# Three transformer blocks with a mixture of experts: two more pieces of expert weights on chip, a top-64 on 32 partitions, wider modulation sums and a final norm by 128 tokens

## The chip, the cores and the metric

The kernel runs on one core of one Trainium2 chip. The metric is device time in microseconds, median of three runs. Engines: PE (matmuls), DVE (vector), ACT (activations, and one queue of DMA issues), POOL (a few vector operations and the indirect gathers), SP (the other queue of DMA issues). A traced execution gives the rows below; its times count from the start of its span.

## The reference, cut to what matters

Two transformer blocks in a row on 512 tokens of width 1024 (mLSTM and MLP, then short convolution and MLP), and then a third with modulation, attention and a mixture of 16 experts. The parts that the diff touches belong to the third:

```
mod = silu(c) @ w_mod + b_mod            # 1024 -> 6144; the same with c_ctx for the context (only 2048 columns are used)
...
x = x + g_a * mix                        # mix = attention output projection
h2 = rmsnorm(x, norm_ffn) * (1 + sc_f) + sh_f
aff = softmax(h2 @ w_router)             # 512 tokens x 16 experts
vals, idx = top_k(aff.T, 64)             # every expert takes its 64 best tokens
xs = h2[idx]                             # 16 x 64 x 1024
y = (silu(xs @ w_gate) * (xs @ w_up)) @ w_down * vals     # per expert: 1024 -> 512 -> 1024
x = x + g_f * scatter_add(y, idx)
return rmsnorm(x, norm_final)
```

All data are float32.

## The kernel before

The program is traced as ordinary loops; a framework then places the instructions on each engine. It takes the instruction that stands first in the program among those that it expects to be ready by its own estimates of durations, so the order on an engine can differ from the program's, and buffers are taken and freed by tag. `keep_in_program_order` pins an instruction.

*Dense stages.* Activations lie with the channels on 128 partitions and 512 tokens on columns. Every weight piece is loaded by SP into `raw`, and split by ACT (L85) and DVE (L86) into a high and a low part `wh`, `wl`; three matmuls (L92 to L94) make one product.

*Modulation (`mods`, L829).* The vector product is not made on PE. For each j of 24 blocks of 256 columns, DVE accumulates 8 slices of `w_mod` times a column of silu(c) into `u` (L877 and L881; twice for the first 8 blocks, since the context needs them too). Loads go in pieces of four slices into tag `b4`. Every four sums, PE adds over partitions with a column block of ones (`rows`), and the sums are turned into columns. The generator's steps are taken between the MLP's blocks, so all this lies beside the matmuls of the first two blocks.

*Attention's output (`attention_out`, L1382).* For each of the 8 channel blocks k: a product, the residual on DVE (L1427), the router's partial sums `stats` on PE (L1402), and the square of x on ACT, added to `acc` by POOL or, for the last two, by DVE (L194, L196). Then `colsum` (L207) makes four columns of sums of squares on PE, `rstd_cols` the reciprocal roots, and L1433 the logits `lg`, with tokens on partitions (4 blocks of 128 tokens, 16 experts each).

*Routing (`route`, L1437).* Softmax; four transposes (L1452) to experts on 16 partitions and 512 tokens on columns, copied into `aT`; eight rounds of the 8 largest values and their replacement by -1 (L1478, L1480); four transposes back (L1485); `sel` marks what was replaced (L1487); triangular and full matmuls (L1489, L1491) count the rank of each token chosen; `rank` (L1494). `onehots` (L1507) compares ranks with 0 to 63, `slots` (L1517) makes each slot's token number, weight and address by matmul, `fetch` (L1529) gathers the 128 token rows of a pair of experts from `h2d` in HBM. Beside this, PE transposes the normalized tokens back to rows (L1472), ACT scales them (L1473) into one tile of tag `ha` and three of tag `wh`, and ACT's queue writes them to `h2d` (L1474).

*Experts (`moe`, L1562).* 8 pairs of experts. Per pair: `feed` transposes the gathered rows (L1573) and modulates them into `xs`; `half` (L1626) makes the gate and up products in halves of four slices, two experts in the two 64-column halves of PE; `inner` (L1632) transposes the activations; `down` (L1605) makes the output of the pair before; `weigh` (L1612, L1613) scales and splits it; `scatter` (L1587, L1588) multiplies with a one-hot and adds into x. The program asks for a pair's second `half` after the scatter of the pair before.

*Expert weights (`moe_loads`, L1532).* 96 pieces of 1 MB (four slices of 512 columns), in the order of use, issued by SP, one buffer each. `mwtags` lists the tags: 10 `mw`, 1 `mx` (that is given back after the routing), 2 `raw`, 2 `mz`. Fifteen pieces are asked for before `route`; the sixteenth takes the first buffer that PE has read, and after `mx` has gone the ring has 14 buffers. The final norm's weights `nf` and a tile `gf` have tag `wh`; `nf` is loaded by ACT's queue (L1675).

*End.* The last pair's output is made in four blocks j of 256 columns with the tokens on partitions (L1595), added to x by two matmuls per 128 tokens, with the high and the low part in turn (L1718, L1719); ACT squares and sums (L1721). Behind the last block: one sum over all four token blocks (L1726), one root (L1727), one reciprocal (L1728), then for each 128 tokens half a row scaled on ACT (L1731), half on DVE (L1732), and a store by SP or ACT's queue (L1733).

Of the kernel before, what the change touches and what calls it, by code (L numbers as in the profile page):

```python
# [18 lines left out]
S = 512  # L19
D = 1024  # L20
# [7 lines left out]
class Net:  # L28
# [800 lines left out]
    def mods(self):  # L829
# [5 lines left out]
        ones = self.c([128, 32], name="ones32")  # L835
        nc.gpsimd.memset(ones, 1.0)
# [24 lines left out]
        for j in range(24):  # L861
            nv = 2 if j < 8 else 1
            if len(sums) % 2 == 0:
                pair = self.t([128, 2, 256], tag="u")
            if nv == 2:
                acc = [pair[:, 0], pair[:, 1]]
            else:
                acc = [pair[:, len(sums) % 2]]
            sums += acc
            for hf in range(2):  # L870
                raw = self.t([128, 4, 256], tag="b4")
                nc.sync.dma_start(raw, a["w_mod_2"][0][hf * 512:(hf + 1) * 512, j * 256:(j + 1) * 256].rearrange("(k p) n -> p k n", p=128))
                for v in range(nv):
                    for k in range(4):
                        c = cs[:, v, hf * 4 + k:hf * 4 + k + 1]
                        if hf + k == 0:
                            o = nc.vector.tensor_scalar(acc[v], raw[:, k], c, None, op0=OP.mult)  # L877
                            if v == 0 and j % 2 == 0:
                                self.tc.keep_in_program_order(o)
                        else:  # L880
                            nc.vector.scalar_tensor_tensor(acc[v], raw[:, k], c, acc[v], op0=OP.mult, op1=OP.add)  # L881
            if j % 2:
                yield
                if len(sums) == 4:
                    t = rows(sums)
                    sums = []
                yield
                if t is not None:
                    columns(t, j, nv)
                    t = None  # L890
# [491 lines left out]
    def attention_out(self, oops):  # L1382
# [22 lines left out]
        for k in range(KD):  # L1405
# [22 lines left out]
            ss.add(self.x[:, k])  # L1428
        stats(KD - 1)
        cols, _ = self.colsum(ss.acc)  # L1430
# [6 lines left out]
    def route(self, cols, lg):  # L1437
# [49 lines left out]
        nc.vector.tensor_scalar(sel, pT[:, 0:64].rearrange("p (c e) -> p c e", c=4), 0.0, None, op0=OP.is_lt)  # L1487
        pp = self.p()[:, 0:64].rearrange("p (c e) -> p c e", c=4)
        nc.tensor.matmul(pp, tri[:, 0], sel, start=True, stop=False, skip_group_check=True)  # L1489
        for c in range(3):  # L1490
            nc.tensor.matmul(pp[:, c + 1:], tri[:, 1], sel[:, c:c + 1].to_broadcast([128, 3 - c, 16]), start=False, stop=c == 2,  # L1491
                             skip_group_check=True)
        rank = self.t([128, 4, 16], tag="rank")
# [5 lines left out]
        for pr in range(2):  # L1499
            self.slots(pr)  # L1500
            self.fetch(pr)
# [326 lines left out]
```

## Time and profile before

| | |
|---|---|
| median of 3 runs | 1812.56 us (1810.69 to 1812.74) |
| profiled execution, own time | 1812.28 us |
| its span | 1810.4 us, 24232 instructions |
| PE busy | 1747.0 us, 96% |
| DVE, ACT, POOL busy | 1009.1 (56%), 680.7 (38%), 80.5 us (4%) |
| chain that ended last | PE 90%, DVE 5%, ACT 3%, DMA 1% |
| moved by DMA | 254.47 MB, mean 141 GB/s |
| mean granted TensorE clock | 0.984 of full speed |

A busy share is a mean over the whole span. In the 40 slices of the page the DMA engines move 48 to 163 GB/s from slice 2 to the attention, 9 to 25 GB/s in most of the attention, and 417 to 420 in four slices of the experts' stage.

### The profile page before, as it was taken

The numbers are of one execution on the slowest core, as the hardware profiler recorded it, in microseconds if no ns is written. First come the engines' busy times: TensorE is split into PE (matmuls) and PEld (weight loads), VectorE is DVE, ScalarE is ACT, GpSimd is POOL, SyncE is SP. The second block draws the span as 40 slices with busy tenths as digits, with TensorE's granted clock in tenths as the row PEclk, the third lists the DMA queues.
The fourth block names the chain that finished last, engine by engine and source line by source line (L and its number), as shares of the span: only waits on it lengthen the run. The fifth ranks groups of instructions, "written<-read, shape, count | busy, mean of one in ns | idle before, by whom it ended". The sixth has DMA issues, their size and how long they took to land.

```text
span 1810.4 us, 24232 instructions
## 1 busy us (share of the span) xinstructions
PE 1747.0 (96%) x9763; PEld 1375.6 (76%) x9763; DVE 1009.1 (56%) x1930; ACT 680.7 (38%) x1228; POOL 80.5 (4%) x100
## 2 busy tenths in 40 slices
PE   7999999999999999999999999989899999799997
PEld 5798898777787888898787878888788887334444
DVE  4554575366756774536455554678776743433332
ACT  4344345333322442244323333344666642111112
POOL 1000000000000000000000001013000001000000
PEclk9899999999999999999999999989999999899999
DMA  6221432244544222322444333220100047799993
GB/s 196 71 70 48 147 110 93 94 140 140 163 140 140 94 93 94 116 93 94 139 140 139 120 105 105 70 75 12 25 13 9 20 142 302 272 419 420 420 417 123
DMA packets 157447, 254.47 MB, mean 141 GB/s; under 512 B 20223, under 2 KB 124056, under 8 KB 145432
## 3 DMA queue, kind: packets, MB, share of 16 engines
q1 hardware_dynamic: 152304, 244.70, 38.7%
q10 hardware_dynamic: 3528, 3.98, 0.7%
q0 software_dynamic: 1504, 4.26, 0.6%
q8 instruction: 76, 1.25, 0.3%
q14 instruction: 35, 0.29, 0.0%
HBM read 248.72 MB, written 4.20 MB: 140 GB/s over the span
## 4 chain that ended last, share of the span: by engine, by line
PE 90%; DVE 5%; ACT 3%; issue 1%; DMA 1%; SPq 0%; DVEq 0%; POOL 0%; ACTq 0%
PE ps L92 22%; PE ps L94 22%; PE ps L93 22%; PE ps L1626 7%; PE ps L1605 3%; PE ps L1185 2%; PE ps L1170 2%; PE pw L1323 1%; PE ps L1588 1%; PE pw L1322 1%; PE ps L1587 1%; ACT wh L85 1%; PE ps L1573 1%; DVE th L301 1%; PE ps L1595 0%
## 5 line engine op out<-in xcount | busy, mean ns | idle before, releaser
L92 PE MATMUL ps<-op,wh 128*128 128x512 f32 (+1 forms) x1808 | 653.3, 367 | 7.0 <-ACT wh L85 2.2
L94 PE MATMUL ps<-op,wl 128*128 128x512 f32 (+1 forms) x1808 | 657.9, 366 | 2.2 <-DVE wl L86 2.2
L93 PE MATMUL ps<-op,wh 128*128 128x512 f32 (+1 forms) x1808 | 658.0, 366 | 0.9 <-DVE op L105 0.7
L86 DVE TENSOR_TENSOR wl<-raw,wh 128x1024 fp32r<-128x1024 f32 x210 | 258.1, 1233 | 256.1 <-ACT wh L85 255.5
L92 PEld LDWEIGHTS ps<-op,wh 128*128 128x128 f32 x1808 | 338.1, 189 | 70.5 <-issue 3.3
L93 PEld LDWEIGHTS ps<-op,wh 128*128 128x128 f32 x1808 | 341.8, 189 | 61.3 <-DVE op L105 1.3
L94 PEld LDWEIGHTS ps<-op,wl 128*128 128x128 f32 x1808 | 341.7, 189 | 60.5 <-DVE wl L86 2.9
L85 ACT CAST wh<-raw 128x1024 fp32r<-128x1024 f32 x210 | 219.9, 1052 | 385.6 <-PE ps L93 350.1
L688 DVE TENSOR_TENSOR t<-t,ps 128x512 f32<-128x512 f32 x96 | 65.8, 686 | 112.0 <-PE ps L94 111.8
L1626 PE MATMUL ps<-mw,xs 128*64 128x512 f32 x400 | 115.3, 600 | 0.0
L881 DVE SCALAR_TENSOR_TENSOR u<-b,csilu,u 128x256 f32<-128x256 f32 x224 | 103.9, 492 | 7.7 <-DMA b<-in_w_mod_dram 3.9
L637 ACT ACTIVATE t<-ps 128x512 f32<-128x512 f32 x64 | 38.0, 594 | 109.0 <-PE ps L94 108.9
L92 PE MATMUL ps<-wh,op 128*128 128x256 f32 x256 | 75.3, 295 | 0.1
L1626 PEld LDWEIGHTS ps<-mw,xs 128*64 128x64 f32 x400 | 33.4, 138 | 52.9 <-issue 50.5
L93 PE MATMUL ps<-wl,op 128*128 128x256 f32 x256 | 72.4, 284 | 0.0
L94 PE MATMUL ps<-wh,op 128*128 128x256 f32 x256 | 71.7, 285 | 0.0
L1140 DVE TENSOR_REDUCE sm<-pw 128x1 f32<-128x768 f32 (+2 forms) x64 | 54.1, 854 | 27.4 <-PE pw L1323 14.2
L196 POOL TENSOR_TENSOR acc<-acc,t 128x512 f32<-128x512 f32 x21 | 28.1, 1337 | 605.4 <-ACT t L194 604.8
L92 PEld LDWEIGHTS ps<-wh,op 128*128 128x128 f32 x256 | 49.1, 192 | 4.2 <-ACT og L532 2.3
L93 PEld LDWEIGHTS ps<-wl,op 128*128 128x128 f32 x256 | 49.0, 192 | 0.2
L1580 DVE TENSOR_SCALAR xs<-ps,Ap 128x128 f32<-128x128 f32 x32 | 13.0, 408 | 64.5 <-PE ps L1573 57.3
L94 PEld LDWEIGHTS ps<-wh,op 128*128 128x128 f32 x256 | 48.3, 191 | 0.1
(467 smaller groups left out, 2158.7 us busy)
## 6 DMA issues: line engine op xcount, KB each, us to landing
raw<-in_w_mlp_up_dram SPq DMA_DIRECT2D x32, 1024.0 KB, 5.5
raw<-in_w_mlp_down_dram SPq DMA_DIRECT2D x32, 1024.0 KB, 5.0
mw<-in_w_gate_dram SPq DMA_DIRECT2D x26, 1024.0 KB, 16.6
b<-in_w_mod_dram SPq DMA_DIRECT2D x48, 512.0 KB, 4.7
mw<-in_w_up_dram SPq DMA_DIRECT2D x24, 1024.0 KB, 18.0
mw<-in_w_down_dram SPq DMA_DIRECT2D x19, 1024.0 KB, 19.9
raw<-in_w_in_conv_dram SPq DMA_DIRECT2D x12, 1024.0 KB, 5.1
raw<-in_w_in_mlstm_dram SPq DMA_DIRECT2D x11, 1024.0 KB, 5.4
```

The lines of the kernel that those rows point to most:

```text
L85: nc.scalar.copy(h, raw[:, k0:k0 + kk])
L86: (eng or nc.vector).tensor_sub(lo, raw[:, k0:k0 + kk], h.bitcast(F32))
L92: mm(out, st[0], mv[0], start=first, stop=False)
L93: mm(out, st[0], mv[1], start=False, stop=False)
L94: mm(out, st[1], mv[0], start=False, stop=last)
L637: nc.scalar.activation(t, src, AF.Relu)
L688: nc.vector.tensor_add(y[i], y[i], p)
L881: nc.vector.scalar_tensor_tensor(acc[v], raw[:, k], c, acc[v], op0=OP.mult, op1=OP.add)
L1140: nc.vector.reduce_max(nm[e], p[e][:, 256:256 + n], axis=AX.X, negate=self.sink is None)
L1170: nc.tensor.transpose(pt[:, x * 128:(x + 1) * 128], self.P[e][:, m * 128:(m + 1) * 128], net.ident)
L1605: nc.tensor.matmul(py[dh][e * 64:e * 64 + 64], aT[:, fh * 2 + f, e * 64:e * 64 + 64], r[e][:, f, dh * 512:dh * 512 + 512], start=fh + f == ...
L1626: nc.tensor.matmul(p[e * 64:e * 64 + 64], xs[:, k, e * 64:e * 64 + 64], r[e][:, k % 4], start=k == 0, stop=k == 7, tile_position=(0, e * 64))
```

## The change

- `mods`: blocks of 512 columns instead of 256 (12 blocks), loads of two slices of 512 columns instead of four of 256, one accumulating instruction over 512 columns. The tile of ones becomes a broadcast of one column.
- `attention_out`: the last block's square is no longer added to `acc`; PE sums the columns of `acc` and of the square into the same four columns.
- `route`: two transposes of 32 columns give 32 partitions (two blocks of 128 tokens, 16 experts each) with 256 columns. Eight maxima and seven replacements give each partition its 64 largest, in falling order. A matmul brings partitions 16 to 31 down to 0 to 15; the maximum of one list with the other reversed holds the 64 largest of both, and its minimum is the expert's threshold. It is spread by a transpose, and `lg` is compared with it: greater, and equal. Ranks are counted for both, those that are equal behind all that are greater.
- `onehots` can be made for two of four experts at a time, so the first pair's slots and gather stand ahead of the second pair's one-hots. `oh` has 4 buffers instead of 8.
- `moe_loads`: two more places in the ring, each of two half pieces: `ha` with `la`, and two of `wh`. They are free when the normalized tokens have been written out. They are used three times (the second place), four times (the first).
- The end: in each block the four matmuls of the high part stand before the four of the low part; sum, root, reciprocal and scaling are made for each 128 tokens.

The diff, cut where only shapes follow from what is shown:

```diff
-        for j in range(24):
+        for j in range(1, 24, 2):
             nv = 2 if j < 8 else 1
...
-            for hf in range(2):
-                raw = self.t([128, 4, 256], tag="b4")
-                nc.sync.dma_start(raw, a["w_mod_2"][0][hf * 512:(hf + 1) * 512, j * 256:(j + 1) * 256].rearrange("(k p) n -> p k n", p=128))
+            for k2 in range(KD // 2):
+                raw = self.t([128, 2, 512], tag="b4")
+                nc.sync.dma_start(raw, a["w_mod_2"][0][k2 * 256:(k2 + 1) * 256, (j - 1) * 256:(j + 1) * 256].rearrange("(k p) n -> p k n", p=128))
...
-                            nc.vector.scalar_tensor_tensor(acc[v], raw[:, k], c, acc[v], op0=OP.mult, op1=OP.add)
+                            nc.vector.scalar_tensor_tensor(o, raw[:, k], c, o, op0=OP.mult, op1=OP.add)
...
-            ss.add(self.x[:, k])
+            if k < KD - 1:
+                ss.add(self.x[:, k])
+        sq = self.t([128, S])
+        nc.scalar.activation(sq, self.x[:, KD - 1], AF.Square)
         stats(KD - 1)
-        cols, _ = self.colsum(ss.acc)
+        pc = self.p()
+        for n, src in enumerate((ss.acc, sq)):
+            for c in range(4):
+                nc.tensor.matmul(pc[:, c:c + 1], src[:, c * 128:(c + 1) * 128], self.ones, start=n + c == 0, stop=n == 1,
+                                 skip_group_check=True)
+        cols = self.rstd_cols(pc[:, 0:4], 4, 1.0 / D)
...
-        for c in range(4):
-            nc.tensor.transpose(pT[0:16, c * 128:(c + 1) * 128], lg[:, c], self.ident)
-        aT = self.t([16, S], tag="aT")
-        nc.vector.tensor_copy(aT, pT[0:16])
+        for i in range(2):
+            nc.tensor.transpose(pT[0:32, i * 128:(i + 1) * 128], lg[:, 2 * i:2 * i + 2].rearrange("p c e -> p (c e)"), self.ident)
+        aT = self.t([32, 256], tag="aT")
+        nc.vector.tensor_copy(aT, pT[0:32, 0:256])
...
-        wk = aT
+        wk, top = aT, self.sm([32, 64])
         for r in range(8):
-            v = self.sm([16, 8])
+            v = top[:, 8 * r:8 * r + 8]
             nc.vector.max(v, wk)
-            nw = self.t([16, S], tag="aT")
-            nc.vector.match_replace(out=nw, in_to_replace=v, in_values=wk, imm_value=-1.0)
-            wk = nw
+            if r < 7:
+                nw = self.t([32, 256], tag="aT")
+                nc.vector.match_replace(out=nw, in_to_replace=v, in_values=wk, imm_value=-1.0)
+                wk = nw
...
-        for c in range(4):
-            nc.tensor.transpose(pT[:, c * 16:c * 16 + 16], wk[:, c * 128:(c + 1) * 128], self.ident[0:16, 0:16])
-        sel = self.t([128, 4, 16], BF, tag="sel")
-        nc.vector.tensor_scalar(sel, pT[:, 0:64].rearrange("p (c e) -> p c e", c=4), 0.0, None, op0=OP.is_lt)
+        nc.tensor.matmul(pT[0:16, 0:64], self.ident[0:32, 16:32], top, start=True, stop=True)
+        m, th = top[0:16], self.sm([16, 1])
+        nc.vector.tensor_tensor(m, m, pT[0:16, 0:64][:, ::-1], op=OP.max)
+        nc.vector.tensor_reduce(th, m, axis=AX.X, op=OP.min)
+        pT = self.p()
+        nc.tensor.transpose(pT[:, 0:16], th.to_broadcast([16, 128]), self.ident[0:16, 0:16])
+
+        sel = self.t([128, 4, 2, 16], BF, tag="sel")
+        T = pT[:, 0:16][:, None, :].to_broadcast([128, 4, 16])
+        nc.vector.tensor_tensor(sel[:, :, 0], lg, T, op=OP.is_gt)
+        nc.vector.tensor_tensor(sel[:, :, 1], lg, T, op=OP.is_equal)
...
+        for c in range(4):
+            nc.tensor.matmul(pp[:, :, 1], tri[:, 1], sel[:, c:c + 1, 0].to_broadcast([128, 4, 16]), start=False, stop=c == 3,
+                             skip_group_check=True)
+        both = self.t([128, 4, 2, 16])
+        nc.vector.tensor_mul(both, pp, sel)
         rank = self.t([128, 4, 16], tag="rank")
-        nc.vector.tensor_mul(rank, pp, sel)
+        nc.vector.tensor_add(rank, both[:, :, 0], both[:, :, 1])
...
-        self.onehots(0)
         for pr in range(2):
+            self.onehots(0, pr)
             self.slots(pr)
             self.fetch(pr)
...
-                raw = self.t(list(ap.shape), tag=self.mwtags.pop(0))
-                nc.sync.dma_start(raw, ap)
-                yield raw
+                tag = self.mwtags.pop(0)
+                if isinstance(tag, str):
+                    raw = self.t(list(ap.shape), tag=tag)
+                    nc.sync.dma_start(raw, ap)
+                    yield [raw[:, i] for i in range(ap.shape[1])]
+                    continue
+
+                n = ap.shape[1] // 2
+                rs = []
+                for i in range(2):
+                    raw = self.t([128, n, ap.shape[2]], tag=tag[i])
+                    nc.sync.dma_start(raw, ap[:, i * n:i * n + n])
+                    rs += [raw[:, j] for j in range(n)]
+                yield rs
...
+            for i, part in enumerate((h, lo)):
+                for c in range(4):
+                    nc.tensor.matmul(X[j // 2 * 4 + c][:, sl], oT[:, c * 128:(c + 1) * 128], part, start=False, stop=i == 1,
+                                     skip_group_check=True)
...
-        ss, cols = self.sm([128, 4]), self.sm([128, 4])
-        nc.vector.reduce_sum(ss, ssq.rearrange("p (c j) -> p c j", j=4), axis=AX.X)
-        nc.scalar.activation(cols, ss, AF.Sqrt, scale=1.0 / D, bias=self.eps)
-        nc.vector.reciprocal(cols, cols)
...
+            ss, col = self.sm([128, 1]), self.sm([128, 1])
+            nc.vector.reduce_sum(ss, ssq[:, c * 4:c * 4 + 4], axis=AX.X)
+            nc.scalar.activation(col, ss, AF.Sqrt, scale=1.0 / D, bias=self.eps)
+            nc.vector.reciprocal(col, col)
...
-        self.open_sb("R0", {"t": 4, "aT": 2, "sel": 1, "tri": 1, "rank": 1, "mv": 1, "tok": 1, "mz": mz, "oh": 8, "xs": 2})
+        self.open_sb("R0", {"t": 4, "aT": 2, "sel": 1, "tri": 1, "rank": 1, "mv": 1, "tok": 1, "mz": mz, "oh": 4, "xs": 2})
...
+        first = ["mw"] * 7 + ["mx"] + ["mw"] * (nm - 7) + ["raw"] * 2 + ["mz"] * mz
+        rest = ["mw"] * nm + ["raw"] * 2 + ["mz"] * mz
+        a, b = [("ha", "la")], [("wh", "wh")]
+        self.mwtags = first + a + b + (rest + a + b) * 2 + rest + a + rest * 4
```

## Rows read from the trace of the kernel before

**Rows 1.** PE's waits from 200 to 1100 us: who for whom, total us, times, longest

```profile
PE ps L94 <- DVE wl L86: 2.2, 3, 1.4
PE ps L92 <- ACT op L308: 1.8, 2, 1.5
```

**Rows 2.** Groups by line and shape on DVE, 200 to 1100 us: busy us, mean ns

```profile
L881 DVE SCALAR_TENSOR_TENSOR u<-b,csilu,u 128x256 f32<-128x256 f32 x224 | 103.9, 492 | 7.7 <-DMA b<-in_w_mod_dram 3.9
```

**Rows 3.** The chain that ended last, around the routing: start us, us, what

```profile
1518.98 0.80 PE ps L1402 x8
...
1525.53 0.76 DVE xres L1427
...
1527.87 1.04 PE ps L207 x8
...
1532.49 1.04 PE ps L1452 x4
...
1534.27 0.69 DVE sm L1478
...
1546.32 0.59 PE ps L1485 x4
...
1547.56 0.23 DVE rank L1494
...
1550.50 4.35 DMA wl<-h2d,slots
```

**Rows 4.** Stretches of the second, fourth and seventh pair: length, engines' busy us, clock, DMA

```profile
1577.20:1604.10 26.90, 26.90 (x126) 11.42 (x127) 6.94 (x12) 4.38 (x8) 0.00 (x0) 1.00 1.01 419
...
1633.20:1662.50 29.30, 29.01 (x126) 12.03 (x126) 10.48 (x19) 4.39 (x8) 0.00 (x0) 1.00 1.01 419
...
1722.10:1752.30 30.20, 29.92 (x135) 12.88 (x134) 9.54 (x17) 5.35 (x10) 0.00 (x0) 1.00 1.01 420
```

**Rows 5.** PE's waits from 1556 us to the end, the longest two of four

```profile
PE ps L1588 <- DVE ys L1613: 1.1, 4, 0.3
PE ps L1718 <- ACT ys L1709: 1.0, 1, 1.0
```

**Rows 6.** PE in order of time, two places between pairs

```profile
1624.41 1.07 PE L1626 MATMUL ps<-mw,xs 128*64 128x512 f32 x2
...
1655.03 0.50 PE L1588 MATMUL ps<-aT,ys 128*128 128x512 f32 x1 [0.29 <-DVE ys L1613]
```

**Rows 7.** Groups by line and shape on DVE, 1522 to 1556 us

```profile
L196 DVE TENSOR_TENSOR acc<-acc,t 128x512 f32<-128x512 f32 x1 | 0.7, 692 | 0.8 <-ACT t L194 0.8
...
L1443 DVE TENSOR_TENSOR sm<-sm,sm 128x64 f32<-128x64 f32 x1 | 0.2, 225 | 0.0
```

**Rows 8.** The instructions of line 757: ns of one, minimum, median, maximum

```profile
L757 DVE SCALAR_TENSOR_TENSOR t<-u,vc,t x8: 744/750/752, 668.5 to 757.4; 128x512 f32<-128x512 f32 x8
```

**Rows 9.** Stretches of the routing, columns as in rows 4

```profile
1542.00:1543.00 1.00, 0.00 (x0) 0.00 (x0) 0.97 (x3) 0.00 (x0) 0.00 (x0) 1.00 0.34 123
1543.00:1546.00 3.00, 0.00 (x0) 0.00 (x0) 2.86 (x7) 0.00 (x0) 0.00 (x0) 0.73 0.96 289
1546.00:1552.00 6.00, 2.73 (x16) 2.50 (x16) 4.27 (x18) 0.00 (x0) 1.20 (x2) 0.50 0.04 17
```

**Rows 10.** SP's issues in order of time, the first behind the routing

```profile
1561.11 0.33 SPq L1550 DMA_DIRECT2D mw<-in_w_down_dram  x1
```

**Rows 11.** ACT's queue in order of time, 1541 to 1543 us

```profile
1541.67 0.34 ACTq L1675 DMA_DIRECT2D wh<-in_norm_final_dram  x1
1542.10 0.39 ACTq L1474 DMA_DIRECT2D h2d<-wh  x1
```

**Rows 12.** DMA issues from 1550.4 to 1551 us: KB each, us to landing

```profile
wl<-h2d,slots POOLq DMA_INDIRECT x1, 4.3
```

**Rows 13.** DMA issues from 1624 to 1630 us

```profile
wl<-h2d,slots POOLq DMA_INDIRECT x2, 10.3
```

**Rows 14.** ACT in order of time, the last 10 us

```profile
1801.57 0.30 ACT L1727 ACTIVATE sm<-sm,eps 128x4 f32<-128x4 f32 x1 [0.24 <-DVE sm L1726]
...
1804.91 0.34 ACTq L1733 DMA_DIRECT2D out_dram<-wl  x1
```

More of the change, by code (lines that the diff above doesn't have):

```diff
@@ L834, in mods @@
         nc.vector.memset(self.mod, 0.0)
-        ones = self.c([128, 32], name="ones32")
-        nc.gpsimd.memset(ones, 1.0)
+        ones = self.ones.to_broadcast([128, 32])
         def rows(acc):
@@ L860, in mods @@
         sums, t = [], None
-        for j in range(24):
+        for j in range(1, 24, 2):
             nv = 2 if j < 8 else 1
[L863 to L869, printed above, removed]
-            for hf in range(2):
-                raw = self.t([128, 4, 256], tag="b4")
-                nc.sync.dma_start(raw, a["w_mod_2"][0][hf * 512:(hf + 1) * 512, j * 256:(j + 1) * 256].rearrange("(k p) n -> p k n", p=128))
-                for v in range(nv):
[L874 to L879, printed above, removed]
-                        else:
-                            nc.vector.scalar_tensor_tensor(acc[v], raw[:, k], c, acc[v], op0=OP.mult, op1=OP.add)
[L882 to L890, printed above, removed]
@@ new lines, in mods @@
+            acc = [self.t([128, 2, 256], tag="u") for _ in range(nv)]
+            sums += [acc[v][:, h] for h in range(2) for v in range(nv)]
+            for k2 in range(KD // 2):
+                raw = self.t([128, 2, 512], tag="b4")
+                nc.sync.dma_start(raw, a["w_mod_2"][0][k2 * 256:(k2 + 1) * 256, (j - 1) * 256:(j + 1) * 256].rearrange("(k p) n -> p k n", p=128))
+                for v in range(nv):
+                    o = acc[v].rearrange("p h n -> p (h n)")
+                    for k in range(2):
+                        c = cs[:, v, k2 * 2 + k:k2 * 2 + k + 1]
+                        if k2 + k == 0:
+                            i = nc.vector.tensor_scalar(o, raw[:, k], c, None, op0=OP.mult)
+                            if v == 0:
+                                self.tc.keep_in_program_order(i)
+                        else:
+                            nc.vector.scalar_tensor_tensor(o, raw[:, k], c, o, op0=OP.mult, op1=OP.add)
@@ L891, in mods @@
+            yield
+            if len(sums) == 4:
+                t = rows(sums)
+                sums = []
+            yield
+            if t is not None:
+                columns(t, j, nv)
+                t = None
         nc.vector.tensor_add(self.mod, self.mod, self.vc[:, 128:176][:, :, None].to_broadcast([128, 48, 2]))
@@ L1497, in route, with onehots @@
         self.slots_all = self.c([128, 8, 8], name="slots")
-        self.onehots(0)
         for pr in range(2):
+            self.onehots(0, pr)
             self.slots(pr)
             self.fetch(pr)
-    def onehots(self, q):
-        self.oh[q] = [self.t([128, 256], F32R, tag="oh") for _ in range(4)]
+    def onehots(self, q, half=None):
+        if not half:
+            self.oh[q] = [self.t([128, 256], F32R, tag="oh") for _ in range(4)]
+        e0, n = (0, 4) if half is None else (2 * half, 2)
         for c in range(4):
             self.nc.vector.tensor_tensor(
-                self.oh[q][c].rearrange("p (e s) -> p e s", s=64),
-                self.tok[:, 1:65][:, None, :].to_broadcast([128, 4, 64]),
-                self.rank[:, c, 4 * q:4 * q + 4][:, :, None].to_broadcast([128, 4, 64]), op=OP.is_equal)
+                self.oh[q][c][:, e0 * 64:e0 * 64 + n * 64].rearrange("p (e s) -> p e s", s=64),
+                self.tok[:, 1:65][:, None, :].to_broadcast([128, n, 64]),
+                self.rank[:, c, 4 * q + e0:4 * q + e0 + n][:, :, None].to_broadcast([128, n, 64]), op=OP.is_equal)
     def slots(self, pr):
@@ L1605, in down @@
                         nc.tensor.matmul(py[dh][e * 64:e * 64 + 64], aT[:, fh * 2 + f, e * 64:e * 64 + 64],
-                                         r[e][:, f, dh * 512:dh * 512 + 512], start=fh + f == 0, stop=fh + f == 2, tile_position=(0, e * 64))
+                                         r[e][f][:, dh * 512:dh * 512 + 512], start=fh + f == 0, stop=fh + f == 2, tile_position=(0, e * 64))
         def weigh(py, val):
@@ L1625, in half @@
                 for e in range(2):
-                    nc.tensor.matmul(p[e * 64:e * 64 + 64], xs[:, k, e * 64:e * 64 + 64], r[e][:, k % 4], start=k == 0, stop=k == 7,
+                    nc.tensor.matmul(p[e * 64:e * 64 + 64], xs[:, k, e * 64:e * 64 + 64], r[e][k % 4], start=k == 0, stop=k == 7,
                                      tile_position=(0, e * 64))
```

11 lines of the change are left out of this document (4 added, 7 removed).

## The prediction

> **What bounds the kernel now.** I read the page first (the chain that ended last is PE for 90%), then the stages in stretches, the waits of PE in each stretch that the diff touches, and the chain through the routing instruction by instruction. The edits touch four stages. The reader should see which work ends last in each.
>
> *Modulation sums* lie under the MLP, convolution and projection matmuls. From 200 to 1100 us PE is named as waiting five times, 2.2 us for DVE's weight splits and 1.8 for a residual's split, never for the sums [rows 1]. DVE spends 103.9 us on the sums there [rows 2], beside PE.
>
> *Routing* is the opposite. From the last projection (DVE at 1525.53) to the first tokens gathered for the experts (1550.50 + 4.35) one chain holds everything: DVE, PE, DVE, gather, PE [rows 3]. Nothing covers it; a microsecond removed from this chain starts the experts a microsecond earlier.
>
> *Experts.* The DMA engines run at 419 GB/s, share 1.01, in every stretch from the second pair on [rows 4], which looks like a stage bound by its loads. But PE's waits in the same stage name no load; the longest sum is 1.1 us for the split of an expert's output [rows 5]. PE is bound by its own instructions, in the order in which they were laid out. That order costs something: the second pair's stretch (each begins behind a pair's first half) took 26.90 us, the fourth 29.30 with the same instructions, the seventh 30.20 with eight transposes more [rows 4]. At the fourth pair's start only two matmuls of the first half run before others come between, and later the scatter stands straight behind the projection that feeds it and waits for DVE [rows 6]. The layout looks like one in which loads were expected late; on the chip they were not late.
>
> *The end* is a chain of square, sum, root, reciprocal, scaling, store.
>
> **The change, part by part.** The sum is made against the profiled execution, 1812.28 us (span 1810.4), which is 0.28 below the median shown. A DVE instruction costs about 1.04 ns per column: (692-225)/(512-64) [rows 7].
>
> 1. *Modulation, 512 columns.* 224 accumulating instructions of 492 ns [rows 2] become 112. The nearest row of 512 columns is 750 ns [rows 8], so 84 us instead of 104. The work stays beside PE: **0**. Bounds: -1, if the waits of rows 1 go, to +1.5, if the longer instruction delays a split that was just in time. If that cover were gone, each of the 112 would cost up to 0.26 us (750 - 492).
>
> 2. *Last square added on PE.* DVE's addition of 512 columns leaves the chain (about 0.7 [rows 7]). But PE now gets two sets of column sums instead of one, at 1.04 each, beside two sets of router sums, at 0.80 [rows 3]. Counted from the last projection's end (about 1525.3), 2 x 0.80 + 2 x 1.04 = 3.7 gives 1529.0; before it was 1527.87 + 1.04 = 1528.9. The addition goes, PE's queue takes its place: **+0.1**. If the last router sums are laid behind the column sums, -0.7; +0.4 at the other end.
>
> 3. *Two transposes for four, and their copy.* 1.04 [rows 3] halves, -0.5; the copy loses 256 columns, -0.27: **-0.8**. Bounds -1.0 and -0.4.
>
> 4. *Top-64 over 256 columns.* The loop runs from 1534.27 to about 1546.18 (0.14 ahead of the next PE row [rows 3]): 11.9 us, 1.49 per round of two full-width passes. 512 columns fewer per round: 1.49 - 2 x 0.27 = 0.95. Seven rounds and one last maximum (0.69 - 0.27 = 0.42): 7.1 us, **-4.8**. Bounds: -4.4, and -6.3 if cost went purely with columns (half, and a replacement less).
>
> 5. *Threshold.* Instead of four transposes (0.59 [rows 3]) there are one matmul, two DVE operations, one transpose and a second comparison. Per small DVE operation 0.23 (as rank [rows 3]) and 0.03 to start, per hop to PE about 0.14 to start and half of the 0.59: -0.3 + 0.44 + 3 x 0.26 = **+0.9**. Bounds +0.5 and +1.6.
>
> 6. *Ranks.* Four more matmuls (0.2, from 0.4 that PE's part took between the transposes' end and rank), 64 more columns (0.07) and an addition (0.26): **+0.5**; bounds +0.3 and +0.9.
>
> 7. *One-hots and slots by pair.* From rank's end (1547.79) to the first gather (1550.50) are 2.7 us [rows 3]. The first gather now needs half the columns of the one-hots and half of the matmuls and copies: **-1.0**, between -0.3 and -1.35. The other halves go beside the gather.
>
> 8. *PE's clock.* PE does nothing from 1542 to 1546; in that time the granted clock falls from 1.00 (2.4 GHz), and it is 0.50 (1.2 GHz) from 1546 to 1552 [rows 9], under all the small matmuls behind the top-64. They now come from about 1541 on, and part of them should still find 2.4 GHz: **-0.3**, between 0 and -0.8.
>
> 9. *Two more megabytes.* Before, the sixteenth load was issued at 1561.11, when PE had read its buffer [rows 10]. Now two pieces (four transfers) start as soon as the normalized tokens have been written out. At the same time the load of the final norm, which sat ahead of the last of these writes on ACT's queue (1541.67 against 1542.10 [rows 11]), has to move behind a later piece, so that write goes out some 1.8 us earlier. Two consequences.
>  (a) The first gather, now issued near 1545.1, may find the DMA engines still busy. The second write had landed by 1541.67, when its buffer was taken again [rows 11], so the pieces start near 1540 to 1541.5; 1 MB of writes that remain (2.5 us at 419 GB/s) and the 2.10 MB (5.0) end near 1547.5. Before, the engines were nearly idle from 1546 to 1552 (share 0.04), so the first 1.5 us of the gather move nothing [rows 9]; about one microsecond of the rest overlaps. Alone it lands in 4.3 us [rows 12], under the full stream in 10.3 [rows 13]. Bounds 0 and +6; nearer to the first: **+1.0**. (The Trainium skill, DMA: Bandwidth & Descriptors, section Queues, rings and completion order, says that each engine goes round the queues packet by packet; two queues would then share evenly and a gather of half a megabyte, 1.25 us of data, would lose 1.25 at worst. The row under load shows 6 lost, so the measurement decides; with the rule's worst case the sum below would be 0.25 later.)
>  (b) The experts' order. PE doesn't wait for loads, so the earlier data by themselves give nothing. What they can change is the layout. It turned from dense to split at the fourth pair's first half, piece 33 of 96 (8 for the first pair, 12 for each later one). If that is where the expected supply ran out, 17 instead of 15 pieces at the start put it off: refilling begins 4 us into the stage and takes time to land, about two pieces' time, so the lead grows from 13 to 15, and 33 x 2/13 = 5 pieces are 0.4 of a pair. A split pair costs 29.30 - 26.90 = 2.4 us: **-1.1**. Bounds: five pairs dense, -12; a worse order, +1.
>
> 10. *Final norm by 128 tokens.* Root, reciprocal and scaling of the first 128 tokens no longer wait for the sum over all (0.2); ACT gets three more roots (0.30 each [rows 14]) between copies, and the last store, issued at 1804.91 [rows 14], may go later. **-0.2**, between -0.5 and +0.6.
>
> Sum: 0 + 0.1 - 0.8 - 4.8 + 0.9 + 0.5 - 1.0 - 0.3 + 1.0 - 1.1 - 0.2 = -5.7, so 1806.6 us. Terms 2 to 9a, the routing, hold -4.4 of it.
>
> **The rivals.**
> *A. The loads, or the order, decide the experts' stage.* If the stage runs at the pace of its loads, two pieces fewer after the start are worth 5.0 us, not 1.1; the time is then 1812.28 - 4.4 - 5.0 - 0.2 = 1802.7, and 1795.7 with five pairs dense. For it: share 1.01 throughout [rows 4]. Against it: no wait for a load [rows 5]. [...]
> *B. The gather pays for the megabytes.* If it still meets most of the stream it lands in 10.3 instead of 4.3: -4.4 + 5.0 - 1.1 - 0.2 = -0.7, so 1811.6: hardly a change. It decides once the two pieces end after about 1549. It is also the case in which the pieces come late and do not do what the change says.
> *C. Slower: the wider sums get in the way of the weight splits.* PE's stages from 200 to 1100 leave little idle; 112 instructions that are 0.26 us longer could add up to 29 us if each delayed a split that PE needs. For: DVE's splits are the one thing PE waits for there [rows 1]. Against: only three such waits, and 20 us less DVE work in all. The kernel is slower when more than 22 of the 112 bite (5.7/0.26); with half of them, 14.6 us: 1821.2.
>
> **Numbers.** Forecast 0.54, A 0.20, B 0.17, C 0.09. About 0.2%, 3.6 us, is what a measurement of this kernel tells from no change: under 1808.7 counts as faster, over 1815.9 as slower. The forecast's own range is 1803.5 to 1810; of its 0.54, 0.45 lie under 1808.7. With A and 0.01 of B: faster 0.66; same 0.09 + 0.16 = 0.25; slower 0.09. The range 1800 to 1812 leaves out C and the lower part of A.
>
> **What would show it.** Right: rounds of 0.95 us in the top-64; column sums that end as late as before relative to the last projection; the first gather 5 to 6 us earlier, landed in about 5; pairs of 27 to 28 us up to the fourth and of 29.5 to 30 after; still no wait of PE for a load. Wrong: a gather of 8 us or more; dense pairs throughout, or more split ones; a wait of PE for a split near the modulation sums; the last store later than 1.5 us behind the first.

## The result, and the profile after

| | before | after |
|---|---|---|
| median, us | 1812.56 (1810.69 to 1813.97) | 1803.53 (1800.58 to 1803.78) |
| ratio | | 0.9947, interval 0.9935 to 0.9958 |
| profiled execution, us (its span) | 1812.28 (1810.4) | 1800.58 (1798.0) |
| from the last residual (DVE) to PE's first transposes of gathered tokens | 29.5 | 28.6 |
| from there to the last pair's inner transposes | 226.0 | 222.8 |
| from there to the end of the span | 29.4 | 29.1 |

Faster by 9.0 us (1806.6 was forecast, the range was 1800 to 1812). The profiled executions differ by more, 11.7, and the extra lies in the first 100 us, in which nothing that was changed runs but for a memset of 0.1 us. The granted clock of 60 to 100 us differs from one execution to the next (columns as in [rows 4]); of the kernel before, then of the kernel after:

```profile
60.00:100.00 40.00, 38.10 (x202) 31.16 (x201) 22.51 (x44) 14.23 (x29) 0.21 (x2) 0.87 0.22 62
```
```profile
60.00:100.00 40.00, 38.13 (x231) 32.82 (x231) 24.36 (x56) 15.17 (x30) 0.21 (x2) 0.96 0.27 79
```

PE's 400th matmul stands at 98.8 us before and at 95.3 after; in the experiments it stands between 93.7 and 98.6, whatever the edit. All comparisons below are made from there, or from the last residual. So counted, the last residual comes 4.6 us earlier (1426.7 against 1422.1 behind the 400th matmul): that is the modulation sums' doing, the only edit ahead of it. With -0.8, -3.2 and -0.3 from the table the parts make -8.9. That this is also the difference of the medians is in part luck: the first part is larger between other executions (term 1 below).

*Modulation.* The group that answers to [rows 2], and PE's waits from 200 to 1100 us, for [rows 1]:

```profile
L876 DVE SCALAR_TENSOR_TENSOR u<-b,csilu,u 128x512 f32<-128x512 f32 x112 | 79.7, 749 | 5.6 <-DMA b<-in_w_mod_dram 4.5
```
```profile
PE ps L92 <- ACT op L308: 1.9, 2, 1.5
PE ps L94 <- DVE wl L86: 0.8, 2, 0.4
```

The 749 ns are those of [rows 8]. (DVE's busy time for the sums goes from 103.9 to 79.7 us; the prediction's 84 adds up single durations, which overlap.) The splits' wait fell from 2.2 to 0.8 us. Where it was lost is seen in the order of time, DVE and POOL of the kernel before:

```profile
230.32 6.35 DVE L881 SCALAR_TENSOR_TENSOR u<-b,csilu,u 128x256 f32<-128x256 f32 x7
236.59 2.35 DVE L86 TENSOR_TENSOR wl<-raw,wh 128x1024 fp32r<-128x1024 f32 x2
```
```profile
230.07 4.24 POOL L196 TENSOR_TENSOR acc<-acc,t 128x512 f32<-128x512 f32 x3 [100.37 <-ACT t L194]
```

Seven sums take 6.35 us where 3.6 would do: three of them took 1.40 us each, one beside each of POOL's additions (1.36), and the split that PE needs stood behind them. DVE had had no idle time since 220 us. The same place after:

```profile
218.42 6.05 DVE L876 SCALAR_TENSOR_TENSOR u<-b,csilu,u 128x512 f32<-128x512 f32 x9
229.28 2.93 DVE L86 TENSOR_TENSOR wl<-raw,wh 128x1024 fp32r<-128x1024 f32 x2 [4.82 <-ACT wh L85]
```

The sums end at 224.47, ahead of POOL's additions (225.96 to 230.0), DVE is idle for 4.8 us, and the split waits for its own input alone.

*Routing.* DVE of the kernel after, in order of time, for [rows 3]:

```profile
1517.44 0.75 DVE L1421 SCALAR_TENSOR_TENSOR xres<-ps,modc,xres 128x512 f32<-128x512 f32 x1 [4.21 <-PE ps L94]
1520.90 0.16 DVE L156 TENSOR_SCALAR sm<-ps 128x4 f32<-128x4 f32 x1 [2.71 <-PE ps L1430]
...
1525.63 0.42 DVE L1482 MAX8 sm<-aT 32x8 f32<-32x256 f32 x1
1526.08 0.08 DVE L1485 MATCH_VALUE_LOAD aT<-sm,aT 32x8 f32 x1
1526.16 0.40 DVE L1485 MATCH_REPLACE8 aT<-sm,aT 32x256 f32<-32x256 f32 x1
...
1535.26 0.22 DVE L1511 TENSOR_TENSOR rank<-t 128x64 f32<-128x64 f32 x1
...
1536.98 0.15 DVE L1539 COPY slots<-ps 128x6 f32<-128x6 f32 x1
```

The slots are ready 19.7 us behind the last residual instead of 24.75 (L1520 is the copy's line in the kernel before):

```profile
1550.13 0.15 DVE L1520 COPY slots<-ps 128x6 f32<-128x6 f32 x1
```

The small matmuls up to the ranks find a granted clock of 1.00 (1532 to 1536 us), where they had 0.50 [rows 9]: the mechanism of term 8.

The rest of that chain: SP's issues of the extra pieces, the last of the four writes on ACT's queue and its landing, POOL's gather and its landing, PE's first use of it:

```profile
1531.40 0.33 SPq L1579 DMA_DIRECT2D ha<-in_w_down_dram  x1
1531.78 1.02 SPq L1579 DMA_DIRECT2D la<-in_w_down_dram  x1
1532.90 2.34 SPq L1579 DMA_DIRECT2D wh<-in_w_up_dram  x2
```
```profile
1531.90 0.33 ACTq L1477 DMA_DIRECT2D h2d<-wh  x1
```
```profile
h2d<-wh ACTq DMA_DIRECT2D x1, 512.0 KB, 6.9
```
```profile
1539.68 1.16 POOL L1548 DMA_INDIRECT wl<-h2d,slots  x1 [14.45 <-DMA wh<-in_w_up_dram]
```
```profile
wl<-h2d,slots POOLq DMA_INDIRECT x1, 6.3
```
```profile
1546.07 1.30 PE L1603 MATMUL ps<-ident,wl 128*128 128x128 f32 x5 [7.78 <-DMA wl<-h2d,slots]
```

The last write goes out right behind its copy, 2.1 us earlier than before against the last residual [rows 11]. But it takes 6.9 us (3.4 in experiment 1, where no piece's load is beside it) and lands at 1538.8. The gather reads what was written, so it goes out 2.5 us behind the slots, and then it needs 6.3 us instead of 4.3 [rows 12]. (The trace names a piece that landed at that moment as the releaser. In the kernels below where it names the write, the gather also goes out 0.9 us behind the write's landing.) Of 5.1 us won, 0.8 are left.

*Experts.* The stretches that answer to [rows 4], and the third between them:

```profile
1568.60:1595.40 26.80, 26.80 (x125) 11.37 (x126) 6.88 (x12) 4.39 (x8) 0.00 (x0) 1.00 1.01 417
1595.40:1623.20 27.80, 27.80 (x134) 12.11 (x133) 11.71 (x29) 4.28 (x8) 1.90 (x2) 1.00 1.02 419
1623.20:1651.10 27.90, 27.90 (x126) 11.39 (x125) 10.58 (x19) 4.39 (x8) 0.00 (x0) 1.00 1.02 417
1709.90:1740.10 30.20, 29.91 (x133) 12.89 (x132) 9.58 (x18) 5.35 (x10) 0.00 (x0) 1.00 1.01 420
```

The third (29.1 before) and the fourth are 1.3 and 1.4 us shorter, the sixth 0.6 (29.4 to 28.8); the others are as before. PE is as full as before, the DMA share is the same, and the layout has changed. Pieces of the chain of waits (start, us, matmuls of the halves in one run), of the kernel before and of the kernel after:

```profile
1604.59 7.02 PE ps L1626 x32
...
1624.48 1.00 PE ps L1626 x2
...
1633.65 4.44 PE ps L1626 x18
```
```profile
1595.94 7.02 PE ps L1656 x32
...
1615.83 3.58 PE ps L1656 x16
...
1623.74 7.02 PE ps L1656 x32
...
1642.65 0.84 PE ps L1656 x2
...
1651.62 4.44 PE ps L1656 x18
```

A stretch that starts with a run of 32 is dense, one that starts with 18 is split. Before, the third pair is the last that starts with 32, and its stretch ends with the fourth pair's first half broken up (2 and 14 instead of 16). After, the same comes one pair later. PE's waits from 1545 us to the end still name no load, apart from the first gather:

```profile
PE ps L1603 <- DMA wl<-h2d,slots: 7.8, 1, 7.8
PE ps L1748 <- ACT ys L1739: 1.7, 1, 1.7
```

*The end.* The last store, for [rows 14]; it stands 5.5 us ahead of the span's end, as before:

```profile
1792.55 0.34 ACTq L1765 DMA_DIRECT2D out_dram<-wl  x1
```

From the last pair's inner transposes to the end of the span the six profiles with the old end take 29.5 us, the seven with the new one 28.8 to 29.4.

### The profile page after: what moved, and what is told of

It is laid out like the page before. It is cut to its first block, busy times and chain, and to the rows that moved or that the text cites. A ratio compares the mean times of both kernels' runs of the same rounds, so it can differ in the third digit from the quotient of the medians.

```text
span 1798.0 us, 24162 instructions
## 1 busy us (share of the span) xinstructions
PE 1737.3 (97%) x9772; PEld 1369.9 (76%) x9772; DVE 979.3 (54%) x1813; ACT 680.6 (38%) x1231; POOL 79.9 (4%) x99
## 3 DMA queue, kind: packets, MB, share of 16 engines
q8 instruction: 76, 1.25, 0.3%
## 4 chain that ended last, share of the span: by engine, by line
PE 90%; DVE 4%; ACT 3%; DMA 2%; issue 1%; SPq 0%; POOL 0%; ACTq 0%; DVEq 0%
PE ps L92 22%; PE ps L93 22%; PE ps L94 22%; PE ps L1656 7%; PE ps L1635 3%; PE ps L1179 2%; PE ps L1164 2%; PE pw L1317 1%; PE ps L1618 1%; PE pw L1316 1%; PE ps L1617 1%; PE ps L1603 1%; ACT wh L85 1%; DVE th L301 1%; PE ps L1625 0%
## 5 line engine op out<-in xcount | busy, mean ns | idle before, releaser
L1656 PE MATMUL ps<-mw,xs 128*64 128x512 f32 x336 | 94.0, 602 | 0.0
L876 DVE SCALAR_TENSOR_TENSOR u<-b,csilu,u 128x512 f32<-128x512 f32 x112 | 79.7, 749 | 5.6 <-DMA b<-in_w_mod_dram 4.5
L637 ACT ACTIVATE t<-ps 128x512 f32<-128x512 f32 x64 | 38.1, 595 | 112.3 <-PE ps L94 112.3
L1656 PEld LDWEIGHTS ps<-mw,xs 128*64 128x64 f32 x336 | 27.5, 138 | 46.3 <-issue 44.2
L196 POOL TENSOR_TENSOR acc<-acc,t 128x512 f32<-128x512 f32 x21 | 27.8, 1325 | 603.4 <-ACT t L194 602.8
L92 PEld LDWEIGHTS ps<-wh,op 128*128 128x128 f32 x256 | 48.4, 189 | 4.2 <-ACT og L532 2.3
L641 DVE CAST op<-t 128x512 fp32r<-128x512 f32 x64 | 27.1, 424 | 38.9 <-ACT t L639 25.3
```

The source lines that it names most:

```text
L92: mm(out, st[0], mv[0], start=first, stop=False)
L637: nc.scalar.activation(t, src, AF.Relu)
L876: nc.vector.scalar_tensor_tensor(o, raw[:, k], c, o, op0=OP.mult, op1=OP.add)
L1656: nc.tensor.matmul(p[e * 64:e * 64 + 64], xs[:, k, e * 64:e * 64 + 64], r[e][k % 4], start=k == 0, stop=k == 7, tile_position=(0, e * 64))
```

## The experiments

The theory after the result: (1) the sums are worth about 4.6 us between the two profiles, because DVE was full beside POOL's additions; (2) the routing is worth its 5 us only as far as the gather's source has been written, and the writes and the gather pay for whatever else is on the DMA queues; (3) the pieces pay through PE's order. Rivals: the loads' pace decides the experts (rival A), the earlier residual is the early clock alone, the routing's steps are worth less than was worked out. Below, "issue" and "feed" are the first gather's issue and PE's first use of it, in us behind the last residual (before 25.0 and 29.5, after 22.2 and 28.6).

**1. The pieces asked for behind the gathers** (PE's order as in the changed kernel):

```
-            self.fetch(pr)
+            self.fetch(pr); pr and self.tc.keep_in_program_order(nc.sync.dma_start(self.sm([128, 1]), self.g[1][:, 0:1]))
...
-        self.route(*logits)
+        self.early = True; self.route(*logits); pre += [next(loads) for _ in range(2)]; self.early = False
```

SP's queue waits at a tiny transfer for the second gather; the pieces' loads stand behind it.

> The changed kernel, but the two extra pieces are asked for right behind the routing and stand on SP's queue behind a small transfer that waits for the second gather; PE's order is unchanged. Theory (the extra loads hold back the last token write, and then the first gather): the gather is issued about 19.7 us after the last residual instead of 22.2 and lands in 4.3 to 5 us instead of 6.3, so the first feed comes 24.2 us after the residual instead of 28.6; the experts' stage is as long as before the edit; total 4.4 us under the changed kernel, near 1799. Rival (the gather waits for something else, or PE needs these pieces early): feed still 28 us behind the residual, or a wait of PE for a load appears; total 1803 to 1806.

1798.33 us, ratio 0.9926 (0.9913 to 0.9938), the fastest of all. It is 5.2 under the changed kernel by the medians, 3.8 by the two ratios and 3.1 by the two profiles behind the 400th matmul. POOL's gather and PE's first use of it:

```profile
1538.06 1.07 POOL L1548 DMA_INDIRECT wl<-h2d,slots  x1 [12.56 <-DVE oh L1526]
```
```profile
1542.67 0.88 PE L1603 MATMUL ps<-ident,wl 128*128 128x128 f32 x3 [3.66 <-DMA wl<-h2d,slots]
```

The gather now waits for DVE, not for a transfer; issue 20.35, landed in 4.5, feed 25.0. The pairs stay (only the fourth rises, 27.9 to 28.5), though their data are asked for 14 us later.

**2. The pieces asked for right behind the writes.** As 1 without the tiny transfer, and the last token tile takes the buffer `ha`:

```
-            t = self.t([128, D], tag="wh" if c else "ha")
+            t = self.t([128, D], tag="wh" if c < 3 else "ha")
```

> The changed kernel, but the last of the four token tiles has the tag ha, so the first extra transfer waits until all four token writes have landed; PE's order is unchanged. Theory: the last write lands in 3.8 us instead of 6.9, the gather is issued 2.5 us earlier, and then shares the engines with 2 MB of loads and lands in 6 to 8 us; feed 26 to 28 us behind the last residual; total 0.5 to 2.5 us under the changed kernel. Rival (the stream under the gather costs nothing, the writes alone count): feed 24.2 us behind, 4.4 us under. Other rival (no contention matters): no difference.

1801.56 us, 0.9942 (0.9929 to 0.9954). The writes are quick again and the gather goes out at 20.35, but it then meets the pieces and lands in 8.5 (6 to 8 expected); feed 29.0, later than in the changed kernel. The times show no difference from it that could be told.

**3. The ring of before** (no extra pieces, all else as changed):

```
-        first = ["mw"] * 7 + ...
+        self.mwtags = ["mw"] * 7 + ["mx"] + ...
```

> The changed kernel with the ring of before (15 pieces ahead, then 14). Theory (contention in the routing and a denser order of PE in the experts are the two effects of the pieces): feed 24 to 25 us behind the last residual instead of 28.6; pairs three and four back to 29.1 and 29.4 us, from 27.8 and 27.9; together 0.5 to 1.5 us under the changed kernel, near 1802.5. Rival (the loads set the experts' pace): every pair near 30 us and the stage 5.0 us longer, total 1804 or more.

1803.62 us, 0.9947 (0.9935 to 0.9960): the changed kernel's time. The pairs are back (29.0, 29.35, 29.3 for the third, fourth and sixth; 3.2 us more in all), and the feed comes 1.9 us earlier (issue 22.0, feed 26.7). It is not the 24 to 25 that was expected: the final norm's load (issued at 1535.0) stands ahead of the last write (1535.5) again, that write lands at 1540.8, and the gather goes out 0.9 us behind it. As placed, the two megabytes bring 3.2 us and cost 1.9 by the traces, and the times show no difference. Rival A's 5 us are not there.

**4. The sums of 256 columns** in the changed kernel (`mods` of before).

> The changed kernel with the modulation sums of 256 columns. Theory (the sums bunch up on DVE where the first MLP begins, and delay the splits that PE needs there): the stretch 220 to 245 us has DVE full again and PE idle for 1.4 us, and the total is 2.4 to 4 us over the changed kernel, 1806 to 1807.5. Rival (DVE is covered there, the difference upstream is the clock of that execution): no difference within 1 us.

1808.43 us, 0.9975 (0.9965 to 0.9985): 4.9 slower than the changed kernel. Again three sums of 1.40 us beside POOL's additions, and PE waits 1.7 us there. Behind that wait the granted clock dips, 0.96 in the stretch where it is 1.00 in both kernels above:

```profile
220.00:260.00 40.00, 38.26 (x265) 35.86 (x264) 30.15 (x64) 17.82 (x38) 4.41 (x3) 0.96 0.38 120
```

Experiment 6, with the same sums, has this dip too, experiments 7 and 9 don't. It costs 1.5 us: behind it the splits stand 1.84 us later than in the kernel before (both behind the 400th matmul), ahead of it 0.36.

**5. The sums of 512 columns alone** in the kernel before.

> The kernel before with the sums of 512 columns alone. If the wider sums are what brings the routing's start forward (the kernel with all parts but these was 4.9 us slower than the changed kernel), this is 4.0 to 5.0 us under the kernel before, with no wait of PE between 225 and 245 us, and the last residual is the same part earlier. If the sums stay beside PE, as the prediction had it, and the earlier residual has another source (the granted clock of the first 100 us), the time is that of the kernel before within 1 us.

1806.16 us, 0.9970 (0.9959 to 0.9981): 5.4 under the kernel before by the ratio, 6.8 by the medians. The last residual is 5.0 us earlier behind the 400th matmul (1421.7), PE's one wait for a split from 200 to 256 us is 0.4; feed 29.4 and pairs as before.

**6. The routing alone** in the kernel before.

> The kernel before with the new routing and the square on PE alone (sums of 256 columns, loads and final norm of before). Prediction: -4.4 to -5.4 us (terms 2 to 8). Theory after the runs so far: the loop and the threshold save their part, but the first gather is then no longer held by the one-hots and waits for the last of the four writes, and the rows come under the load of other transfers, so -2 to -3 us. Rival, that the routing brings nothing: within 1 us.

1810.98 us, 0.9992 (0.9984 to 1.0001), which does not exclude no change. Issue 22.9, landed in 4.5, feed 27.5. ACT's queue:

```profile
1542.26 0.34 ACTq L1692 DMA_DIRECT2D wh<-in_norm_final_dram  x1
1542.69 0.39 ACTq L1475 DMA_DIRECT2D h2d<-wh  x1
```

The load of the final norm still sits ahead of the last write; it waits for a buffer, and the write, whose data were ready at 1540.7, goes out 2.0 us late. Before, the slots came later than the written tokens; now they don't.

**7. The extra pieces alone** in the kernel before.

> The kernel before with the extra pieces on chip alone (routing, sums and final norm of before). If the gain of the experts' stage (3.2 to 3.5 us over the pairs) hangs on the pieces and the gather, asked for about 3 us later here, is as quick as before, the time is 2.5 to 3.5 us under the kernel before. If the pieces take from the gather what they bring to the experts' stage here too, as in the changed kernel, it is within 1 us. Prediction: 1.0 lost at the gather and 1.1 won in the pairs, so within 1 us as well; the pairs and the gather's landing tell these two apart.

1809.16 us, 0.9982 (0.9974 to 0.9991), 3.3 under by the ratio. Issue 25.0 and feed 29.5, as before; pairs of 27.9, 27.9 and 28.8: the gather, 3 us later than in the changed kernel, finds most of the pieces landed and takes 4.4 us.

**8. Without POOL's additions of squares** in the kernel before. They are left out in every norm that sums so, and the norms' values are not the reference's.

```
-            eng.tensor_add(o, o, sq)
+            if eng is nc.vector:
+                eng.tensor_add(o, o, sq)
```

> The kernel before without GpSimd's additions of squares to the sum of squares (they are left out in every norm that sums so, and the norms' values are not the reference's; VectorE's own additions stay). If GpSimd's additions are what stretched three of the modulation's VectorE instructions from 0.48 to 1.40 us at 230 to 235 us, none of these takes over 0.6 us here, PE's wait of 1.39 us at 237.9 us for the weight split is gone, and the time is 1.4 to 2.5 us under the kernel before. If VectorE was stretched by its own reads or by transfers, three instructions of 1.4 us stay, and the time is that of before within 0.7 us.

The place of the seven sums:

```profile
229.80 3.61 DVE L882 SCALAR_TENSOR_TENSOR u<-b,csilu,u 128x256 f32<-128x256 f32 x7
233.33 2.36 DVE L86 TENSOR_TENSOR wl<-raw,wh 128x1024 fp32r<-128x1024 f32 x2
```

None takes over 0.5 us, and PE's wait of 1.4 us there is gone (one of 0.4, some 25 us later, is in both kernels): POOL's additions were what stretched them. The splits stand 135.0 us behind the 400th matmul (98.3) instead of 137.8; in the changed kernel 134.0. The time, 1811.51 (0.9996, 0.9987 to 1.0005), is 0.7 to 1.4 less: at the low end of what was expected, and not told from no change.

**9. The routing alone, the final norm's load behind the last write:**

```
+            d = nc.scalar.dma_start(hd[c], t)
+            if c == 3:
+                self.tc.keep_in_program_order(d)
...
+                self.tc.keep_in_program_order(nc.scalar.dma_start(nf, a["norm_final_2"].partition_broadcast(128)))
```

> As the run with the new routing alone, and the final norm's load moved behind the last of the four writes on ScalarE's queue. There the routing gave 1.9 us, and its first gather waited for the last write, which went out 2.0 us after its copy. If that load ahead of the last write is what held the gather, the write goes out right behind its copy, the gather is issued 20.4 to 21.2 us behind the last residual (22.9 there, 25.0 before), lands in 4.3 to 5, and the time is 3.5 to 4.5 us under the kernel before: the prediction's terms 3 to 8 come out whole. If the writes take their time for another reason, the gather is issued no earlier than 22.5 and the time is that of the routing alone within 0.7 us.

1806.62 us, 0.9968 (0.9956 to 0.9981): 4.4 under the routing alone. By the traces 3.0 of it are the gather's: it waits for DVE, issue 19.8, feed 24.4, which is 5.0 earlier than before. What else separates the two executions (1.4 us between the 400th matmul and the last residual, 0.9 behind the feed) has no edit to it. It goes with PE's clock: from 220 to 260 us it was 0.96 in experiment 6 and 1.00 here, and behind the feed PE stayed at 1.2 GHz for 5.0 us there and for 3.1 here.

**10. One extra piece instead of two:**

```
-        self.mwtags = first + a + b + (rest + a + b) * 2 + rest + a + rest * 4
+        self.mwtags = first + a + (rest + a) * 3 + rest * 4
```

> The changed kernel with the first extra piece only (one megabyte more on chip instead of two). If the experts' gain comes from PE's order (with one extra piece the second and third pair already stand with 16 matmuls of the first half in one run, as in the changed kernel, where the kernel without pieces has 1 and 7, or 9 and 7), the pairs are 27.8 and about 27.9 to 28.5, then 30.1, 29.3 and 30.2, 2.5 to 3 us under those without extra pieces. If it comes from the amount of data on chip, half of the gain goes: 1.6 to 1.8 us. The gather meets one megabyte less than in the changed kernel: issued at 20.4 to 22 us behind the last residual, landed in 4.5 to 6. Time 1 to 2 us under the changed kernel.

1804.65 us, 0.9952 (0.9938 to 0.9966). Half of the expectation held. Pieces of the chain of waits, the starts of the fourth pair's stretch and of the fifth's:

```profile
1628.06 7.02 PE ps L1656 x32
...
1655.97 4.44 PE ps L1656 x18
```

The third and the fourth pair are dense: 27.8 and 27.9, the sixth 29.3. One megabyte brings 2.6 of the 3.2 us, by the order, not by the amount. The gather went against what was expected: issue 25.2, feed 29.9. Here the final norm's load stays ahead of the last write, and both take twice their time among the pieces' loads (ACT's queue, and landing times):

```profile
1534.48 0.34 ACTq L1705 DMA_DIRECT2D wh<-in_norm_final_dram  x1
1534.91 0.40 ACTq L1477 DMA_DIRECT2D h2d<-wh  x1
```
```profile
wh<-in_norm_final_dram ACTq DMA_DIRECT2D x1, 512.0 KB, 8.0
h2d<-wh ACTq DMA_DIRECT2D x1, 512.0 KB, 8.7
```

**11. The last square added by DVE** in the changed kernel (`attention_out` of before).

> The changed kernel with the last square added by VectorE again and one set of column sums behind it. Prediction: 0.1 us better than the changed kernel (term 2). By the two traces: the column sums end 3.4 instead of 2.6 us behind the last residual, and the gather, which waits for the writes, goes later by the same 0.8. Both are within what the times can tell; the stretch from the last residual to the column sums' end decides between them.

1802.87 us, 0.9946 (0.9933 to 0.9960), no difference to be told. From the last residual to DVE's first use of the column sums: 3.41 here, 3.46 in the changed kernel, 3.41 before. The second reading in the expectation was a misreading of the trace: it took the sums over `acc` for the last, but those over the square come last.

## Why the prediction was right, and by which errors

The sign, the range and the forecast's side held; the sum (-5.7) was 3.2 short, for three mis-sized terms that partly cancel. That the range held is therefore partly luck: 1803.53 lies at the very edge of the forecast's own range (1803.5 to 1810) and nearer to rival A's 1802.7, whose mechanism is excluded below. Of the signs the rounds of 0.95 us, the pairs up to the fourth and the absence of a wait for loads came true; the first gather went out 2.7 us earlier, not 5 to 6. One slip in the sum is harmless: 0.4 of a pair at 2.4 us is 1.0, not 1.1.

| term | forecast | measured |
|---|---|---|
| 1 modulation | 0 | -4.6 |
| 2 square on PE | +0.1 | +0.1 |
| 3 transposes, copy | -0.8 | -0.6 |
| 4 top-64 | -4.8 | -4.8 |
| 5, 6, 8 threshold, ranks, clock | +1.1 | +1.1 |
| 7 one-hots by pair | -1.0 | -0.85 |
| 9a gather | +1.0 | +4.2 |
| 9b order in the experts | -1.1 | -3.2 |
| 10 final norm | -0.2 | -0.3 |

Terms 2 to 8 are read between DVE rows of the two traces (last residual, first use of the column sums, first maximum, end of the loop, rank, slots): -5.1 of -5.4. The round of the loop took 0.96 us (forecast 0.95), which confirms the cost per column in [rows 7] for maximum and replacement too; experiment 9 shows the steps in the time.

*Term 1 failed.* "The work stays beside PE" held on the mean and not at 230 us, where DVE was full, stretched by POOL, and the split was late. The wait stood in [rows 1] (the longest, 1.4, is this one), and the bound of -1 took such waits for all that could be won. Experiment 4 shows 4.9 us in the time, experiment 5 5.0 in the trace.

The 4.6 of the table is at the low end. Behind its 400th matmul the last residual stands at 1426.7 to 1428.8 us in the five profiles with the sums of 256 columns and POOL's additions, the kernel before being the earliest of them, and at 1421.1 to 1422.3 in the seven with 512.

Experiment 8 shows the cause for part of it: of the 3.8 us by which these splits are earlier after, 2.8 vanish with POOL's additions alone; from 276 us on that is 1.7 of 2.7, and at the last residual 0.9 of 4.6. About 2 us more build up between 276 us and the last residual, most of them behind 1131 us, where no such sum runs any more: from there to the last residual the seven profiles take 391.6 to 392.2 us and the five 393.2 to 394.4. Of the two kernels compared, part of it is PE's clock, 0.83 before and 0.89 after from 1185 to 1215 us, or 1.8 us at full clock. Why it differs, and the rest, stays open.

Rival C looked at the same edit and had the wrong sign: fewer, longer instructions clear DVE earlier. The Trainium skill, SBUF — State Buffer, section Who interferes with whom, says that a DVE instruction with two inputs in SBUF contends with a GpSimd instruction that reads SBUF, and that the one that comes second waits. The trace agrees: 0.48 us became 1.40 beside additions of 1.36.

*Term 9a failed in place and size.* The prediction priced the gather's own transfer (+1.0) and let the write go out earlier. It did not ask what the new slots' time meets: the gather's source. 2.3 of the 4.2 us are the wait for the last write, which shares the engines with the pieces; 1.9 are the slower gather, between the forecast and rival B (6.0). Without the pieces' loads beside it, it took 4.5 (experiments 1 and 9); right behind the pieces' issue, 8.5 (experiment 2). The Trainium skill, DMA: Bandwidth & Descriptors, section Queues, rings and completion order, says that each engine goes round the queues packet by packet; were the turns even, the gather would lose 1.25 at most, by the prediction's estimate. The 4.0 between experiments 1 and 2 go against that reading once more.

*Term 9b: right mechanism, size off.* PE waits for no load and the layout turns from dense to split later. The prediction let two more pieces put the turn off by 0.4 of a pair; it came a whole pair later, which made the third and the fourth stretch shorter, and one piece was enough for that (experiment 10). That the loads' pace decides is excluded: data that come 14 us later leave the pairs nearly as they are (experiment 1), and share 1.01 goes with no wait.

## What to carry to other kernels

When a chain is shortened, look for its second input: the new end of the chain meets transfers that used to be early, and a prefetch put into the freed gap is charged to them. Ask for the prefetch behind the transfer that the chain waits for (here 3 to 5 us for one pinned transfer); 0.5 MB that are wanted at once and megabytes that are wanted later do not belong on the engines at the same time. And "it lies beside PE" is a statement about every window: find the places where that engine is full, and who else is on it or beside it there.

## What was not expected of the hardware

- A DVE accumulation of 256 columns went from 0.48 to 1.40 us beside a POOL addition.
- A write of 0.5 MB landed in 3.0 to 3.5 us ahead of the pieces' loads (changed kernel, experiments 1 and 2; the DMA share was 0.91 to 1.02 there, so the engines were not free), in 6.9 with loads of pieces beside it, in 8.7 in experiment 10; a gather of 0.5 MB in 4.3 to 4.6 without them, in 6.3 and 8.5 with them.
- The granted clock of 60 to 100 us was 0.87, 0.96 and (experiment 5) 1.00 in executions of the same work, worth up to 5 us; PE was busy for 38.1, 38.1 and 37.9 of 40 us in them, so its own business does not say why. That is open.
